# A decoder layer on one core: delays of the norm chains, an overlap of two of them, and the place of a weight cast

## The chip, the core and the metric

The kernel runs on one core of a Trainium2 chip. A core has five engines, each with its own instruction stream: TensorE (PE: matrix products, with weight loads shown apart as PEld), VectorE (DVE), ScalarE (ACT), GpSimd (POOL) and SyncE (SP), whose stream here mostly issues DMA transfers. An engine runs its stream in order and waits on semaphores for the others. The metric is the device time of one execution in microseconds; smaller is better.

## What is computed

One inference step of one decoder layer, for a prompt of 1024 tokens and a sample group of 8 x 8 = 64 tokens that share the weights; together 1088 columns of 1024 values. All data is float32.

```python
def rmsnorm(x, g):
    y = x32 * lax.rsqrt(jnp.mean(x32 * x32, axis=-1, keepdims=True) + NORM_EPS)
    return (y * g.astype(jnp.float32)).astype(x.dtype)
def swiglu(x, w_gu, w_down):
    gate, up = jnp.split(x @ w_gu, 2, axis=-1)
    return (jax.nn.silu(gate) * up) @ w_down
def macaron_half(x, g_pre, w_gu, w_down, g_post):
    return x + 0.5 * rmsnorm(swiglu(rmsnorm(x, g_pre), w_gu, w_down), g_post)
...
hp = macaron_half(hp, ffn1_...)                       # FFN 1, width 2752
fq, fk, fv, lf, gq, gk, gv, gg, la = project(rmsnorm(hp, mix_norm_pre[l]), w_in[l], ...)
fo = fox_prompt(fq, fk, fv, lf)                       # forgetting attention, 8 heads x 64
go, s_p = gla_prompt(gq, gk, gv, la)                  # gated linear attention, 4 heads
hp = hp + rmsnorm(merge(fo, go, gg, gla_norm[l], w_out[l]), mix_norm_post[l])
hp = macaron_half(hp, ffn2_...)                       # FFN 2
```

The sample group goes through the same layer, with a paged cache of keys and values for its attention. Outputs are both groups' results and the new keys, values, gates and states.

## The kernel before

Activations lie transposed: 128 features to a partition block, eight blocks `k` (`KB`), tokens along the free axis. Tokens are cut into the chunks `CH` (0-256, 256-512, 512-768, 768-1088). Weights come through a `Feed`: a DMA brings a raw tile `wr`; ScalarE casts it to a high part `wh`, VectorE subtracts to get a low part `wl` (line 202 for both), and a product is three matmuls, `wh` by the activations' high part (`ua`, `ub`, `hh`), `wh` by the low part (`hl` and the like) and `wl` by the high part (line 219). `Feed.pump(ahead)` casts ahead of need; `ahead` is by default `NW` = 3 tiles, counted from the last one given free, and raw loads run ahead of the casts by `NRAWW` = 2.

The stages on TensorE in order, by the span's time: FFN 1 in two halves of the columns (to about 770 us); the combined projection of the first 512 columns, with units of 128 outputs each (770 to 935); the same for the other columns with attention interleaved (to 1126, the rest to 1219); the product with `w_out`, which runs among the last units; FFN 2 of the first half, with the sample group's paged attention beside it; and FFN 2 of the second half, from about 1890 to the end, in a form with seven products instead of eight for each pair of blocks (`job_seven`, the "sevens").

The order is set when the program is built. The main line is a list of jobs. Beside it run generators, the side chains: each `yield d` asks to be taken up again `d` microseconds later on a planner's clock, which counts the matmuls emitted (`tick`). One list, `quick`, is stepped whenever due; of the other, `side`, only the first entry is stepped, so the chains in it follow one another. What is emitted at a step takes its place in the engines' order close to where the main line then stands.

A norm chain (`norm`) is such a generator: squares on ScalarE, their sum `ss` on VectorE and GpSimd (line 318), a product with ones that gives a column of sums `ncol` (line 333), the power -1/2 on GpSimd, a diagonal `dg` on VectorE (line 375), a product with ones that spreads it over all rows, `nrows` (line 382), and then eight multiplications, each with its residual (lines 422 and 423) or its split into high and low parts (lines 445 to 448). A chain with `post` and `pre` does both norms one after the other. `DROWS` = 2 is the delay between diagonal and `nrows`, `DREDUCE` = 6 the one ahead of the second `ncol`. The chain behind FFN 1 has the key "p"; the chain `w0` between the `w_out` product and FFN 2 has the key "f2", and `first` of FFN 2 waits for it chunk by chunk (`need`).

A projection unit's result leaves its PSUM bank by `proj_evac`. For the value heads of both attentions ("V units") ScalarE copies it to a staging tile `st` (line 932; a ring of five), the chain yields, then TensorE turns it by transposes (line 937), and copies and DMAs follow (lines 944 and 955).

In the sevens the eighth step of a pair (`third`) adds the product to `sg` (line 696), which empties a PSUM bank, and for the last block of a group the operations silu, product, `hh` and `hl` follow (lines 705 to 709). The down products come next; VectorE adds their banks to `y` (line 629).

Of the kernel before, what the change touches and what calls it, by code (L numbers as in the profile page):

```python
# [33 lines left out]
NW = 3  # L34
# [4 lines left out]
STEP = 2.0  # L39
DREDUCE = 6.0  # L40
DROWS = 2.0
COL = 0.42e-3


# [125 lines left out]
class Step:  # L170
    def __init__(self, ctx, tc, A, O):
        self.ctx, self.tc, self.nc, self.A, self.O = ctx, tc, tc.nc, A, O
        nc = self.nc
        self.const = ctx.enter_context(tc.tile_pool(name="const", bufs=1))
        self.dram = ctx.enter_context(tc.tile_pool(name="dram", bufs=1, space=DRAM))
        self.n = 0
        self.side, self.quick, self.bg, self.pend = [], [], [], []
        self.ncw, self.ssb, self.xb = NCW, 3, 2
        self.ready = set()
        self.kept, self.later = False, []  # L180
        self.last, self.pin = {}, True
        self.calm, self.haste = False, 0.0
        self.held = False
        self.rate = self.due = self.now = 0.0
        self.banks = dict(col=("col", 1), col2=("col", 1), rows=("rows", 1))
        cp = self.const
        self.ident = cp.tile([P, P], F32, name="ident")
        make_identity(nc, self.ident)
        self.ones = cp.tile([P, P], F32, name="ones")
        nc.vector.memset(self.ones, 1.0)  # L190
        self.mhalf = cp.tile([P, 4], F32, name="mhalf")
        nc.vector.memset(self.mhalf, -0.5)
        self.gain = cp.tile([P, 6, KB], F32, name="gain")
# [193 lines left out]
        while key not in self.ready:  # L387
            self.step_side(True)

    def norm(self, y, y0, c0, n, pool, post=None, pre=None, v=None, key=None):  # L390

        nc = self.nc
        rows = lambda k: y[:, k, c0 - y0:c0 - y0 + n]
        if v is None:
            sums = []
            for k in range(KB):
                self.square(rows(k), k, n, pool, sums)
            v = [self.rms(sums, n, pool, "col2")]
        if post:
            gi, res, out = post  # L400
            xs = []

            def fetch():
                k = 2 * len(xs)
                if k < KB:
                    xs.append(pool.tile([P, 2, self.ncw], F32, name=self.uid("x"), tag="x", bufs=self.xb))
                    nc.sync.dma_start(xs[-1][:, :, :n], res[:, k:k + 2, c0:c0 + n])
            for _ in range(self.xb):
                fetch()
        while not v:  # L410
            yield
        yield self.haste / 3 or 2.0
        dg = self.rms_diag(v[0], pool)
        yield self.haste / 3 or DROWS
        if post:
            rb = self.rms_rows(dg, n)
            self.held = self.haste > 0
            sums = []
            for k in range(KB):
                if k and k % 2 == 0:  # L420
                    yield
                nc.vector.scalar_tensor_tensor(out=rows(k), in0=rows(k), scalar=self.gain[:, gi, k:k + 1], in1=rb[:, :n], op0=ALU.mult, op1=ALU.mult)
                (nc.gpsimd if k % 2 else nc.vector).tensor_tensor(out=rows(k), in0=rows(k), in1=xs[k // 2][:, k % 2, :n], op=ALU.add)
                if k % 2:
                    fetch()
                if k % 4 == 3:
                    s = slice(k - 3, k + 1)
                    nc.sync.dma_start(out[:, s, c0:c0 + n], y[:, s, c0 - y0:c0 - y0 + n])
                if pre is not None:
                    self.square(rows(k), k, n, pool, sums)  # L430
            if pre is None:
                self.ready.add((key, c0))
                return
            yield DREDUCE
            v = self.rms(sums, n, pool, "col2")
            yield 1.0
            dg = self.rms_diag(v, pool)
            yield DROWS
        rb = self.rms_rows(dg, n)
        xh, xl, o = self.at(c0)  # L440
        for k in range(KB):
            if k and k % 2 == 0:
                yield
            yk = rows(k)
            nc.vector.scalar_tensor_tensor(out=yk, in0=yk, scalar=self.gain[:, pre, k:k + 1], in1=rb[:, :n], op0=ALU.mult, op1=ALU.mult)
            uh, ul = xh[:, k, o:o + n], xl[:, k, o:o + n]
            nc.scalar.copy(uh, yk)
            (nc.gpsimd if k % 2 else nc.vector).tensor_tensor(out=ul, in0=yk, in1=uh.bitcast(F32), op=ALU.subtract)
        self.ready.add((key, c0))
# [73 lines left out]
    def ffn(self, w_gu, w_dn, f):  # L523
# [168 lines left out]
        def job_seven(g, hb, i, z, w):  # L692

            n = f.n // 2
            a, b = slice(0, n), slice(n, 2 * n)
            add = lambda out, x, y: self.keep(nc.vector.tensor_tensor(out=out, in0=x, in1=y, op=ALU.add))  # L696
            if i == 0:
                if hb == g[0]:
                    make(g)
                sg(hb)  # L700
                z.up = f.H.tile([P, 2 * n], F32, name=self.uid("up"), tag="up", bufs=1)
                z.turn, self.kept = 0, True
                z.q, z.u, z.v = f.temps
            t, up = sgs[hb], z.up
            silu = lambda c: self.keep(nc.scalar.activation(out=t[:, c], in_=t[:, c], func=AF.Silu))
            mul = lambda c: self.keep(nc.vector.tensor_tensor(out=t[:, c], in0=t[:, c], in1=up[:, c], op=ALU.mult))
            hh, hl = hid[hb]
            high = lambda c: self.keep(nc.scalar.copy(hh[:, c], t[:, c]))
            low = lambda c: self.keep(nc.vector.tensor_tensor(out=hl[:, c], in0=t[:, c], in1=hh[:, c].bitcast(F32), op=ALU.subtract))  # L709
            whole, last = slice(0, 2 * n), hb == g[-1]  # L710
            self.calm = not last and i >= 2
            if i == 0:
                seven(z, w, 0, "b11", lambda ps: self.keep(nc.scalar.copy(z.q, ps)))
                seven(z, w, 1, "t2", lambda ps: add(z.u, z.q, ps))
            elif i == 1:
                seven(z, w, 1, "t3", lambda ps: add(z.v, z.u, ps))

                def both(ps):
                    add(z.u, z.u, ps)
                    add(up[:, b], z.v, ps)  # L720
                seven(z, w, 0, "t1", both)
            elif i == 2:
                def first(ps):
                    add(t[:, a], z.q, ps)
                    if last:
                        silu(a)
                seven(z, w, 0, "b21", first)

                def second(ps):
                    add(up[:, a], z.v, ps)  # L730
                    if last:
                        for fn in (mul, high, low):
                            fn(a)
                seven(z, w, 1, "t4", second)
            else:
                def third(ps):
                    add(t[:, b], z.u, ps)
                    if last:
                        for fn in (silu, mul, high, low):
                            fn(b)  # L740
                    else:
                        self.later += [lambda fn=fn: fn(whole) for fn in (silu, mul, high, low)]
                seven(z, w, 0, "b22", third)
            self.flush()
# [51 lines left out]
        for g, chunks, kind in f.plan:  # L796
# [8 lines left out]
            elif kind == "last":  # L805
                up4 = [gu(2 * hb - 1 + i) for hb in g for i in range(2)]
                dn = [[w_dn[d2][:, 2 * P * g[0]:2 * P * (g[-1] + 1)] for d2 in d] for d in ((0, 1), (2, 3))]
                reqs = up4[:3] + [(r, f.place(i)) for i, r in enumerate([up4[3]] + dn)]
# [26 lines left out]
    def work(self, jobs):  # L835
        self.feed = Feed(self, [r if isinstance(r, (tuple, Sums)) else (r, None) for rs, *_ in jobs for r in rs])
        for reqs, fn, early in jobs:
            ws = [self.feed.get() for _ in reqs]
            self.feed.pump()
            fn(*ws)  # L840
            self.feed.free(len(reqs) - early)
        self.flush()


# [25 lines left out]
class StepA(Step):  # L870
# [35 lines left out]
    def proj_evac(self, u, c0, n, pt):  # L906
# [8 lines left out]
        elif u < U_GATE:  # L915
            i = u - U_FQ if u < U_FK else u - U_FK
# [13 lines left out]
        elif U_FV <= u < U_GG or u >= U_GV:  # L930
            s = st(F32)
            nc.scalar.copy(s[:, :n], pt)
            yield 3.0
            tp = self.mm(512)
            bl = blocks(c0, n)
            for j, (o, w) in enumerate(bl):
# [4 lines left out]
            if u >= U_GV:  # L941
                i = u - U_GV
# [8 lines left out]
            else:  # L951
                i = u - U_FV
# [8 lines left out]
        else:  # L961
            i, dst, sc = (u - U_GQ, self.gqs, 0.125) if u < U_GK else (u - U_GK, self.gks, 1.0)
# [358 lines left out]
class StepB(StepA):  # L1321
# [432 lines left out]
    def whole(self):  # L1754
# [19 lines left out]
        y0 = F.tile([P, KB, HALF], F32, name="y0")  # L1774
# [164 lines left out]

        jobs += j2[:UNITS0] + [([], start3, 0)] + j2[UNITS0:]  # L1940
        j3 = self.proj_jobs(ORDER1, lambda j: CH[2:], hook3)
        w0 = Part(y0=0, after=lambda c0, n, v: self.norm(p3.y, 0, c0, n, w0.N, (3, self.h1, self.h2), 4, v, "f2"))
        p4 = Part()

        def mid3():
# [122 lines left out]
f='float32'  # L2068
# [37 lines left out]
```

## Time and profile before

| | us |
|---|---|
| median of 3 runs (lowest to highest) | 2300.27 (2299.33 to 2301.25) |
| profiled execution | 2296.98 |
| its span | 2295.2 |
| TensorE busy | 2233.1 (97%) |
| VectorE busy | 1523.3 (66%) |
| ScalarE busy | 1017.9 (44%) |
| GpSimd busy | 685.6 (30%) |

The mean granted clock of TensorE was 0.994 of full speed. Times in the views are counted from the span's start. A row of the timeline gives start, duration, engine, line, operation, output and inputs, the count where several are put together, and in brackets the idle time ahead with the instruction that ended it. Line numbers in the rows are those of the kernel before.

### The profile page before, as it was taken

What the parts mean: (1) busy time and instruction counts of PE and PEld (TensorE: products, weight loads), DVE (VectorE), ACT (ScalarE), POOL (GpSimd) and SP (SyncE); (2) the same over time, 40 slices, a digit from 0 to 9 for tenths busy, and PEclk for the clock granted to TensorE, in tenths of its full rate; (3) what the DMA queues carried; (4) which work ended last, traced back from release to release, by engine and by line L of the source; (5) the groups of instructions that cost most, each with busy time, mean ns of one, the idle gap of its engine ahead of it and who ended that gap; (6) DMA issues with size and microseconds to landing.
All of it is one profiled execution on the core that took longest, in us unless ns stands there. A gap on an engine that the chain in (4) does not pass through costs nothing.

```text
span 2295.2 us, 40073 instructions
## 1 busy us (share of the span) xinstructions
PE 2233.1 (97%) x15004; PEld 1984.3 (86%) x15004; DVE 1523.3 (66%) x2670; ACT 1017.9 (44%) x1748; POOL 685.6 (30%) x639
## 2 busy tenths in 40 slices
PE   7999999999999999999999999999999999999999
PEld 6998898999999877889897667777777989999998
DVE  7677787877778774576345333348774688778766
ACT  5443444533344565655344312236555545334432
POOL 3333332432223231011323444731110134334413
PEclk9999999999999999999999999999999999999999
DMA  6233333322334566563556899875545554234324
GB/s 212 87 97 93 105 102 120 102 79 92 93 111 138 184 226 192 174 191 122 187 154 211 293 328 307 294 211 147 149 137 152 183 178 127 93 96 134 106 79 138
DMA packets 199427, 357.22 MB, mean 156 GB/s; under 512 B 27265, under 2 KB 102594, under 8 KB 198850
## 3 DMA queue, kind: packets, MB, share of 16 engines
q1 hardware_dynamic: 187570, 316.38, 44.0%
q0 software_dynamic: 11664, 38.28, 4.9%
q8 instruction: 119, 1.95, 0.3%
q14 instruction: 74, 0.61, 0.1%
HBM read 308.93 MB, written 45.65 MB: 154 GB/s over the span
## 4 chain that ended last, share of the span: by engine, by line
PE 72%; DVE 12%; issue 6%; ACT 4%; DMA 4%; POOL 2%; SPq 1%; DVEq 0%; POOLq 0%; ACTq 0%
PE mm L219 45%; PE mm L681 14%; DVE wl L202 4%; PE mx L681 2%; PE po L1428 1%; ACT wh L202 1%; PE sp L1169 1%; PE po L1207 1%; PE tp L1412 1%; PE pa L1561 1%; PE s L1394 1%; DVE qd L1520 1%; DVE hl L709 1%; PE s L1395 1%; DVE fm L1399 0%
## 5 line engine op out<-in xcount | busy, mean ns | idle before, releaser
L219 PE MATMUL mm<-ua,wh 128*128 128x512 f32 (+1 forms) x1488 | 459.6, 392 | 3.2 <-ACT ua L202 1.8
L202 DVE TENSOR_TENSOR wl<-wr,wh 128x1024 fp32r<-128x1024 f32 (+1 forms) x249 | 290.6, 1167 | 174.3 <-ACT wh L202 172.1
L202 ACT CAST wh<-wr 128x1024 fp32r<-128x1024 f32 (+1 forms) x249 | 245.6, 986 | 312.8 <-PE mm L219 228.7
L219 PE MATMUL mm<-ub,wh 128*128 128x320 f32 (+2 forms) x1600 | 332.2, 302 | 0.0
L219 PE MATMUL mm<-hl,wh 128*128 128x256 f32 (+2 forms) x1006 | 331.0, 331 | 0.1
L219 PE MATMUL mm<-hh,wh 128*128 128x256 f32 (+2 forms) x958 | 320.8, 337 | 7.9 <-DVE sg L696 4.6
L219 PEld LDWEIGHTS mm<-ua,wh 128*128 128x128 f32 x1488 | 269.6, 193 | 64.6 <-issue 16.3
L219 PE MATMUL mm<-hh,wl 128*128 128x256 f32 (+2 forms) x958 | 316.6, 331 | 2.2 <-DVE wl L202 2.2
L219 PE MATMUL mm<-ua,wl 128*128 128x512 f32 (+1 forms) x736 | 281.2, 383 | 0.4 <-DVE wl L202 0.4
L219 PEld LDWEIGHTS mm<-ub,wh 128*128 128x128 f32 (+1 forms) x1600 | 255.3, 189 | 6.2 <-issue 4.4
L681 PE MATMUL mm<-ub,wh 128*128 128x288 f32 (+1 forms) x1328 | 258.3, 290 | 0.0
L219 PE MATMUL mm<-ub,wl 128*128 128x320 f32 (+1 forms) x784 | 232.0, 296 | 0.0
L629 DVE TENSOR_TENSOR y<-y,mm 128x256 f32<-128x256 f32 (+2 forms) x275 | 137.1, 525 | 119.7 <-PE mm L219 118.8
L681 PEld LDWEIGHTS mm<-ub,wh 128*128 128x128 f32 x1328 | 210.9, 189 | 0.0
L219 PEld LDWEIGHTS mm<-hh,wh 128*128 128x128 f32 x958 | 180.8, 189 | 30.0 <-DVE sg L696 5.9
L219 PEld LDWEIGHTS mm<-hl,wh 128*128 128x128 f32 x1006 | 189.8, 189 | 15.2 <-issue 1.1
L219 PEld LDWEIGHTS mm<-hh,wl 128*128 128x128 f32 x958 | 181.0, 189 | 19.4 <-DVE wl L202 3.7
L681 PE MATMUL mm<-ub,wl 128*128 128x288 f32 (+1 forms) x664 | 192.8, 290 | 0.0
L681 PE MATMUL mm<-ua,wh 128*128 128x288 f32 (+1 forms) x912 | 177.6, 290 | 0.0
L219 PEld LDWEIGHTS mm<-ua,wl 128*128 128x128 f32 x736 | 141.4, 193 | 28.8 <-issue 2.7
L1088 POOL DMA_INDIRECT pr<-in_cv,rows x128 | 129.7, 1013 | 106.9 <-PE sp L1169 32.0
L219 PEld LDWEIGHTS mm<-ub,wl 128*128 128x128 f32 x784 | 148.0, 189 | 0.2 <-issue 0.2
(324 smaller groups left out, 4229.5 us busy)
## 6 DMA issues: line engine op xcount, KB each, us to landing
wr<-in_wgu SPq DMA_DIRECT2D x72, 512.0 KB
wr<-in_wd SPq DMA_DIRECT2D x68, 512.0 KB
pr<-in_ck SPq DMA_DIRECT2D x112, 256.0 KB
wz<-in_wgu SPq DMA_DIRECT2D x100, 256.0 KB
wr<-in_win SPq DMA_DIRECT2D x50, 512.0 KB
wx<-in_wgu SPq DMA_DIRECT2D x50, 256.0 KB
wr<-in_wout SPq DMA_DIRECT2D x24, 512.0 KB
wr<-in_wd SPq DMA_DIRECT2D x40, 256.0 KB
```

What stands on the lines that cost most here:

```text
L202: for ins in (self.nc.scalar.copy(hi, src), self.nc.vector.tensor_tensor(out=lo, in0=src, in1=hi.bitcast(F32), op=ALU.subtract)):
L219: ins = self.nc.tensor.matmul(*a, **kw)
L629: self.note(nc.vector.tensor_tensor(out=yk, in0=yk, in1=pds[d2, c0, e], op=ALU.add))
L681: nc.tensor.matmul(ps, a, x, start=(k == 0 and j == 0), stop=(k == KB // 2 - 1 and j == len(ops) - 1))
L709: low = lambda c: self.keep(nc.vector.tensor_tensor(out=hl[:, c], in0=t[:, c], in1=hh[:, c].bitcast(F32), op=ALU.subtract))
L1088: nc.gpsimd.indirect_dma_start(out=raw[:, i], out_offset=None, in_=A["ck" if kind == "K" else "cv"].rearrange("g p n -> (g p) n"), in_offs ...
L1169: nc.tensor.matmul(sp[32 * a:32 * a + 32, 256 * hf:256 * hf + 256], qz[p % 2][:, a, s, :], raw[:, :, a * P:(a + 1) * P], start=False, stop ...
L1207: nc.tensor.matmul(po[r], pT[:, t, r], raw[:, :, a * P:(a + 1) * P], start=(t == 0), stop=False)
L1394: nc.tensor.matmul(sp[:, o:o + m], qa[:, qs], ka[:, o:o + m], start=True, stop=False)
L1395: nc.tensor.matmul(sp[:, o:o + m], qb[:, qs], kb[:, o:o + m], start=False, stop=not end)
L1412: nc.tensor.transpose(tp[:, k * P:(k + 1) * P], p[:, (k0 + k) * P:(k0 + k + 1) * P], self.ident)
L1428: nc.tensor.matmul(out, v[:, k, r], pT[:, k, s], start=(k == 0 or (k == 1 and not one)), stop=(k == last or (k == last - 1 and not one)))
```

## The change

Four things change. A norm chain with key "p" waits `DPROJ` = 4 planner microseconds between diagonal and `nrows`, both times, in place of 2. V units wait 5 in place of 3 between copy and transposes. The chain `w0` gets `over`: after the first norm's results are out, it moves the next chain that waits in `side` over to `quick`, so that the second chunk's chain is stepped beside the rest of the first. And at the last block of a group's step 2 (`second`), in the half with `f.end`, `pump` and `free` look ahead `NW - 1` = 2 tiles only, so that one cast pair is emitted a job later.

```diff
+DPROJ = 4.0
...
+        self.near = None
...
-    def norm(self, y, y0, c0, n, pool, post=None, pre=None, v=None, key=None):
+    def norm(self, y, y0, c0, n, pool, post=None, pre=None, v=None, key=None, over=False):
...
-        yield self.haste / 3 or DROWS
+        rest = DPROJ if key == "p" else DROWS
+        yield self.haste / 3 or rest
...
+            if over and len(self.side) > 1:
+                self.quick.append(self.side.pop(0))
             yield DREDUCE
...
-            yield DROWS
+            yield rest
...
             self.calm = not last and i >= 2
+            self.near = NW - 1 if f.end and last and i == 2 else None
...
-            self.feed.pump()
+            self.feed.pump(self.near)
             fn(*ws)
-            self.feed.free(len(reqs) - early)
+            self.feed.free(len(reqs) - early, self.near)
...
             nc.scalar.copy(s[:, :n], pt)
-            yield 3.0
+            yield 5.0
...
-        w0 = Part(y0=0, after=lambda c0, n, v: self.norm(p3.y, 0, c0, n, w0.N, (3, self.h1, self.h2), 4, v, "f2"))
+        w0 = Part(y0=0, after=lambda c0, n, v: self.norm(p3.y, 0, c0, n, w0.N, (3, self.h1, self.h2), 4, v, "f2", True))
```

No instruction is added or taken away on any engine apart from the program's own bookkeeping; rows change their places. Three places follow. Line numbers of the changed kernel are up to six higher.

The first is VectorE in the second group of the last FFN half, from the last block's first adds to the first down tile's banks (`wl` is a weight tile's low part, `y` the FFN's output). Before:

```order
L709 TENSOR_TENSOR hl_20985<-sg_21386,hh_20984 128x288
L202 TENSOR_TENSOR wl_21494<-wr_21422,wh_21493 128x1024
L696 TENSOR_TENSOR sg_21386<-y_9261,mm_21508 128x288
L706 TENSOR_TENSOR sg_21386<-sg_21386,up_21387 128x288
L709 TENSOR_TENSOR hl_20985<-sg_21386,hh_20984 128x288
L202 TENSOR_TENSOR wl_21527<-wr_21459,wh_21526 128x1024
L629 TENSOR_TENSOR y_19338<-y_19338,mm_21530 128x256
```

After:

```order
L714 TENSOR_TENSOR hl_20985<-sg_21386,hh_20984 128x288
L701 TENSOR_TENSOR sg_21386<-y_9261,mm_21493 128x288
L711 TENSOR_TENSOR sg_21386<-sg_21386,up_21387 128x288
L714 TENSOR_TENSOR hl_20985<-sg_21386,hh_20984 128x288
L204 TENSOR_TENSOR wl_21512<-wr_21422,wh_21511 128x1024
L204 TENSOR_TENSOR wl_21516<-wr_21459,wh_21515 128x1024
L634 TENSOR_TENSOR y_19338<-y_19338,mm_21530 128x256
```

The first of the two casts moved from between the two columns' operations to behind both, and the two casts now stand next to each other ahead of the `y` add.

The second is TensorE where the projection ends (`ub` operands) and FFN 2 begins (`mm_13430`, `ua` operands), with the second chunk's `ncol` and `nrows`. Before:

```order
L219 MATMUL mm_13329<-ub_104,wl_13193 128x320
L333 MATMUL ncol_2158_13380<-ones,ss_13242 128x2 x2
L219 MATMUL mm_13430<-ua_99,wh_13284 128x256
L219 MATMUL mm_13430<-ua_100,wh_13284 128x256
...
L382 MATMUL nrows_13388<-dg_13386,ones 128x128 x2
L219 MATMUL mm_13430<-ua_99,wl_13285 128x256
```

After:

```order
L221 MATMUL mm_13207<-ub_104,wl_13037 128x320
L335 MATMUL ncol_2140_13239<-ones,ss_13003 128x2 x2
L221 MATMUL mm_13207<-ub_104,wh_13036 128x320
...
L384 MATMUL nrows_13293<-dg_13265,ones 128x128 x2
L221 MATMUL mm_13285<-ub_104,wh_13166 128x320
...
L221 MATMUL mm_13430<-ua_99,wh_13329 128x256
```

Before, `ncol` stood directly ahead of the FFN's first matmul and `nrows` eight matmuls inside it. Now `ncol` stands 99 gemm matmuls ahead of that first matmul and `nrows` 69, and 30 lie between the two.

The third is ScalarE in the first projection, where the last chunk's norm (squares, lines 314 and 316) meets the first V unit's copy (`st`, lines 932 and 938). Before:

```order
L314 ACTIVATE sq_8899<-y_113 128x320
L314 ACTIVATE sq_8907<-y_113 128x320
L920 ACTIVATE st_8920<-mm_8843 128x512
L926 COPY st_8926<-mm_8843 128x512
L314 ACTIVATE sq_8955<-y_113 128x320
L314 ACTIVATE sq_8960<-y_113 128x320
L202 CAST wh_9029<-wr_8914 128x1024
L314 ACTIVATE sq_8977<-y_113 128x320
L314 ACTIVATE sq_8984<-y_113 128x320
L932 COPY st_8997<-mm_8916 128x512
L955 COPY st_9017<-mm_9011 128x512
```

After:

```order
L926 ACTIVATE st_8893<-mm_8831 128x512
L204 CAST wh_8952<-wr_8829 128x1024
L932 COPY st_8899<-mm_8831 128x512
L316 ACTIVATE ss_8941<-y_113 128x320
L316 ACTIVATE ss_8935<-y_113 128x320
L938 COPY st_8962<-mm_8889 128x512
L204 CAST wh_9017<-wr_8887 128x1024
L316 ACTIVATE sq_8966<-y_113 128x320
L316 ACTIVATE sq_8974<-y_113 128x320
```

The V unit's copy stood behind all eight squares of the chunk and stands now behind the first two. On TensorE the chain's `nrows` moved 27 matmuls of 512 columns later there, and the V unit's four transposes 9 of them later; the next chain's `nrows` (the second norm of the same chunk) comes 38 matmuls later.

## The prediction

> **What bounds the kernel now.** I read the page first, then TensorE's waits in total, then the timelines around the largest of them. The page's head, busy times and granted clock:
>
> ```profile
> span 2295.2 us, 40073 instructions
> PE 2233.1 (97%) x15004; PEld 1984.3 (86%) x15004; DVE 1523.3 (66%) x2670; ACT 1017.9 (44%) x1748; POOL 685.6 (30%) x639
> PEclk9999999999999999999999999999999999999999
> ```
>
> TensorE is busy for 2233.1 of 2295.2 us. The kernel is bound by it nearly everywhere, and no rearrangement that leaves the matmuls as they are can win more than the 62.1 us of idle time plus what short half-clock stretches cost. So the question is which of its waits the change touches. The view of TensorE's waits (microseconds in total, how often, longest one):
>
> ```profile
> PE nrows L382 <- DVE dg L375: 5.8, 4, 2.4
> PE mm L219 <- DVE sg L696: 4.6, 4, 1.8
> PE ncol L333 <- DVE ss L318: 4.6, 4, 1.9
> PE mm L937 <- ACT st L932: 2.6, 1, 2.6
> PE mm L219 <- DVE y L629: 1.3, 2, 1.1
> PE s L1394 <- DMA ka<-ks: 1.2, 1, 1.2
> ```
>
> These are small lists: four times a norm's `nrows` product waited for VectorE's diagonal, four times a norm's `ncol` for its sum, four times a down product for VectorE to empty a bank (`sg` L696), once a transpose for ScalarE's copy. The change works on just these. A result counts as no change within 0.2%, which is 4.6 us and about what a measurement of this kernel can tell.
>
> **The change part by part.**
>
> *Cast of the second down tile (`near`).* It acts on the five groups of the last FFN half (the only one with `f.end`). TensorE's rows at the four groups that wait, and in the second one what VectorE and ScalarE do around it:
>
> ```profile
> 1964.30 0.41 PE L219 MATMUL mm<-hh,wh 128*128 128x320 f32 x1 [1.13 <-DVE sg L696]
> 2036.52 0.41 PE L219 MATMUL mm<-hh,wh 128*128 128x320 f32 x1 [0.63 <-DVE sg L696]
> 2110.09 0.41 PE L219 MATMUL mm<-hh,wh 128*128 128x320 f32 x1 [1.76 <-DVE sg L696]
> 2181.93 0.41 PE L219 MATMUL mm<-hh,wh 128*128 128x320 f32 x1 [1.13 <-DVE sg L696]
> ...
> 2033.91 0.46 DVE L709 TENSOR_TENSOR hl<-sg,hh 128x288 fp32r<-128x288 f32 x1 [0.50 <-ACT hh L708]
> 2034.87 1.23 DVE L202 TENSOR_TENSOR wl<-wr,wh 128x1024 fp32r<-128x1024 f32 x1 [0.50 <-ACT wh L202]
> 2036.02 0.44 DVE L696 TENSOR_TENSOR sg<-y,mm 128x288 f32<-128x288 f32 x1
> 2038.88 1.23 DVE L202 TENSOR_TENSOR wl<-wr,wh 128x1024 fp32r<-128x1024 f32 x1 [0.49 <-ACT wh L202]
> 2040.02 1.14 DVE L629 TENSOR_TENSOR y<-y,mm 128x256 f32<-128x256 f32 x3
> ...
> 2033.79 1.05 ACT L202 CAST wh<-wr 128x1024 fp32r<-128x1024 f32 x1
> ...
> 2040.49 0.39 PE L219 MATMUL mm<-hh,wh 128*128 128x256 f32 x1
> ```
>
> The bank that TensorE needs is emptied by the add at 2036.02. That add stands on VectorE behind the cast of 1.23 us, and the cast waited 0.50 for ScalarE's half of it. The four waits add up to 1.13 + 0.63 + 1.76 + 1.13 = 4.65 us. With the cast gone from there, the add can follow the operation of 2033.91 directly. The cast's row and the add's overlap by 2034.87 + 1.23 - 2036.02 = 0.08; with the same overlap the add would start at 2033.91 + 0.46 - 0.08 = 2034.29, which is 1.73 earlier, and the wait goes.
>
> What is late next: both casts now stand in a row behind the block's last operation, ahead of the `y` add that empties the banks of the first down tile. The cast at 2038.88 would start 1.73 earlier, at 2037.15; two of them, at the 1.14 from start to start that the rows of 2038.88 and 2040.02 show, put the `y` add at 2037.15 + 2 x 1.14 = 2039.43, only 0.59 earlier than now. TensorE's next down tile starts at 2040.49, on the heels of that add. So a group gains some 0.59 and not its whole wait; 4 x 0.59 = 2.4 us. The ends are 4.65 (the bank freed at 2040.02 turns out not to be needed at once) and 0 (ScalarE's two casts come later than I assume). I take 2.4, since the rows of 2040.02 and 2040.49 stand so close. The fifth group has no such wait and costs nothing.
>
> *Two norm chains overlap (`over`, ahead of the second FFN).* TensorE, then VectorE, then two stretches with the granted clock (the third number from the end):
>
> ```profile
> 1219.72 0.61 PE L333 MATMUL ncol<-ones,ss 128*128 128x2 f32 x4 [1.30 <-DVE ss L318]
> 1221.92 1.04 PE L382 MATMUL nrows<-dg,ones 128*128 128x128 f32 x4 [0.54 <-DVE dg L375]
> ...
> 1219.24 0.43 DVE L318 TENSOR_TENSOR ss<-ss,sq 128x256 f32<-128x256 f32 x1
> 1221.35 0.43 DVE L375 TENSOR_TENSOR dg<-ident,nv 128x256 f32<-128x256 f32 x1 [0.82 <-POOL nv L364]
> ...
> 1222.10:1225.60 3.50, 3.50 (x18) 3.50 (x18) 3.10 (x7) 0.41 (x1) 0.00 (x0) 0.51 0.41 109
> 1225.60:1229.00 3.40, 3.40 (x31) 3.40 (x31) 1.26 (x4) 2.79 (x8) 1.65 (x3) 1.00 0.39 95
> ```
>
> The second chunk's chain now ends directly ahead of the FFN's first product, with nothing left for TensorE to do meanwhile: 1.30 + 0.54 = 1.84 us of idle time, and behind it 3.5 us at a clock of 0.51, in which 18 matmuls ran where the next 3.4 us hold 31. Those 18 would have taken 18 x 3.4 / 31 = 2.0, so the half clock cost about 1.5. Afterwards the chain's `ncol` has 99 gemm matmuls behind it before the FFN starts, and 30 of them stand between it and its `nrows`; at 3.4 / 31 = 0.11 us each `ncol` comes some 11 us ahead of the FFN, and the 30 between the two last 3.3 us, more than the 1221.92 - 1219.72 = 2.2 that the chain took from the one to the other. Cover: the rest of the projection. I count the whole, 1.84 + 1.5 = 3.3 us; the ends are 3.3 and 0 (a chain that waits as long in its new place).
>
> [...]
>
> *Rows and turning with more delay in the first projection (`DPROJ`, and 5 for 3 in `proj_evac`).* TensorE, VectorE and ScalarE:
>
> ```profile
> 822.88 0.91 PE L382 MATMUL nrows<-dg,ones 128*128 128x128 f32 x6 [2.04 <-DVE dg L375]
> 838.01 0.66 PE L937 MATMUL mm<-ident,st 128*128 128x128 f32 x4 [2.62 <-ACT st L932]
> 838.96 0.40 PE L219 MATMUL mm<-ua,wl 128*128 128x512 f32 x1
> 839.66 0.39 PE L219 MATMUL mm<-ua,wl 128*128 128x512 f32 x1
> ...
> 821.65 1.08 DVE L375 TENSOR_TENSOR dg<-ident,nv 128x384 f32<-128x384 f32 x1
> ...
> 836.65 0.83 ACT L314 ACTIVATE sq<-y 128x320 f32<-128x320 f32 x2 [1.32 <-DVE st L1014]
> 837.39 0.57 ACT L932 COPY st<-mm 128x512 f32<-128x512 f32 x1
> ```
>
> Three matmuls of 512 columns take 839.66 - 838.96 = 0.70, 0.233 each. The order puts `nrows` 27 of them later (12 of the unit it stood in and 15 of the next), 6.3 us; the diagonal was ready 2.04 too late, so some 4 us of slack remain. The first transposes move 9 matmuls later, 2.1 us, and their copy (837.39, which stood behind eight squares of the norm that themselves waited for VectorE) now has only the first two squares ahead of it. Both waits should go: 2.04 + 2.62 = 4.66 us. The ends are 4.7 and 0 (ScalarE's copy late again). I take 4.7: each cover is twice the wait or better.
>
> What is queued behind: the last norm chain's `nrows` comes 38 matmuls later in the order, 38 x 0.233 = 8.9 us, less the 4.7 won, so about 4.2 later in time. It holds a buffer pool that the attention's tiles take over. GpSimd's clearing, the queue's first load behind it and the next wait:
>
> ```profile
> 860.96 2.17 POOL L1356 CAST kb<-zero 64x512 fp32r<-64x512 f32 x2
> ...
> 868.85 0.42 SPq L1327 DMA_DIRECT2D gnorm<-in_gnorm  x1
> 874.13 0.59 SPq L1375 DMA_DIRECT2D kb<-ks  x1
> ...
> 876.28 0.47 PE L1394 MATMUL s<-ka,qa 128*128 128x128 f32 x2 [1.17 <-DMA ka<-ks]
> ```
>
> Clearing would end at 863.13 + 4.2 = 867.3; SP's load of `kb` would be due at 874.13 - 4.7 = 869.4. SP's order up to there is set by the weight tiles and is nearly the old one, so it moves with TensorE. Hidden by 2.1 us, which is thin.
>
> *The same delay in the two chains of FFN 1's tail.* The rows it moves past:
>
> ```profile
> 728.58 0.42 PE L219 MATMUL mm<-hh,wh 128*128 128x320 f32 x1 [1.08 <-DVE y L629]
> 740.71 0.58 PE L333 MATMUL ncol<-ones,ss 128*128 128x2 f32 x4 [0.68 <-DVE ss L318]
> ```
>
> These may vanish (+1.76). But the chains' eight multiplications and splits now fall on other down products, whose banks VectorE empties; a wait of the kind at 728.58 can come back once per chain, 2 x 1.08 = 2.2. Between +1.8 and -2.2 I take 0.
>
> *The other V units* (the delay holds for all) change TensorE's order by a few rows without a wait that I can see to go: 0, bounded by the slower rival below. DMA counts, matmul counts and queues' loads are the same; SP's rows move by a few places.
>
> **Sum.** 2.4 + 3.3 + 4.7 + 0 = 10.4 us. The profiled execution took 2296.98 us (span 2295.2 and 1.8 around it), 3.3 below the median of 2300.27; 2296.98 - 10.4 = 2286.6 there, and 2300.27 - 10.4 = 2289.9 for the median.
>
> **The rivals.** *What the projection wins is given back at the next load.* If the last chain slips by the 2.1 us more that the clearing has in hand, the loads behind it on SP hold TensorE at the row now at 876.28, whose wait grows from 1.17 by up to 4.7. For it: that wait exists already. Against it: SP's rows are paced by weight tiles. Gain 5.7, time 2294.6.
>
> *The half clock stays, or returns elsewhere.* The wait goes but a stretch of 0.51 is met at some other place: 1.5 less, 2291.4; twice, 2292.9. For it: the stretches follow short gaps, and other gaps stay.
>
> *The waits only move.* The chains wait just as long in new places, and the casts alone count: 2297.9, no change. For it: VectorE is 66% busy and a chain's length is its own. Against it: the counted matmuls above.
>
> *Slower: the staging ring.* A V unit holds one of the five `st` buffers from its copy to its transposes, now for 2 us more of planned time. If that makes a later unit's copy late, TensorE waits for the bank:
>
> ```profile
> L932 ACT COPY st<-mm x24: 367/428/588, 837.4 to 1192.0; 128x512 f32<-128x512 f32 x8, 128x256 f32<-128x256 f32 x8, 128x320 f32<-128x320 f32 x8
> ```
>
> 24 copies at up to 0.588 us: one such wait each is 24 x 0.59 = 14.2, against a gain of 10.4, that is +3.8: 2304.1. From 0.63 us a unit on, the kernel is slower by over 0.2%. Against it: only the first of the 24 had a wait for ScalarE of over 2 us, and the others fall where TensorE waits little.
>
> **How the numbers follow.** Forecast 0.50; loads give it back 0.18; half clock 0.10; waits only move 0.14; ring 0.08. The forecast and the half clock are faster; the loads' case at 2294.6 lies 1.1 inside the limit of 2295.7, so I count 0.10 of its 0.18 as faster and 0.08 as no change; the ring is slower. Faster 0.70, same 0.22, slower 0.08. The best case is 4.65 + 3.3 + 4.7 + 1.8 = 14.5, or 2285.8; I start the range at 2285.5. Upward it takes in the loads' case and waits that only move, 2297.9 with 1 us of room: 2299. Outside stay the ring and a little of each other case. The forecast's own range, with the small parts at their ends, is 2286 to 2293.
>
> **What would show it.** Right: no wait for `sg` in the four groups, and the `y` add about 0.6 us earlier behind its group's first down product; no `ncol` or `nrows` wait between 1210 and 1220, and a clock of 1.00 there; no wait at the last chunk's `nrows` and the first V transposes. Wrong: a wait for `y` of a microsecond in the four groups, a wait for `ka` or `kb` of over 3 us, a row with `st` behind many transposes, or new waits for `y` in FFN 1's tail.

## The result, and the profile after

The changed kernel's median is 2292.41 us (2291.40 to 2294.12, 7 runs) against 2300.27 (2295.55 to 2301.25, 7 runs): 0.9976 of the time before, interval 0.9967 to 0.9986. That is 7.9 us between the medians; by the ratio, which is not formed from these two medians, it is 5.5 us, and 3.2 to 7.6 by the interval. The interval's lower end lies inside the 4.6 us that the prediction counts as no change. The forecast was 2289.9. The profiled execution's span is 2290.5 us, 4.7 less than before. The page's head:

```profile
span 2290.5 us, 40083 instructions
PE 2231.0 (97%) x15004; PEld 1983.1 (87%) x15004; DVE 1532.2 (67%) x2670; ACT 1016.9 (44%) x1748; POOL 690.1 (30%) x639
```

TensorE runs the same 15004 matmuls and is still the bound. What changed is its list of waits (us, times, longest):

```profile
PE mm L221 <- DVE y L634: 6.4, 11, 1.3
PE nrows L384 <- DVE dg L377: 3.9, 2, 2.4
PE ncol L335 <- DVE ss L320: 3.2, 2, 2.5
PE mm L221 <- ACT wh L204: 1.6, 2, 1.3
PE s L1400 <- DMA ka<-ks: 1.2, 1, 1.2
PE mm L221 <- ACT st L955: 1.0, 1, 1.0
PE mm L943 <- ACT st L938: 0.9, 1, 0.9
PE mm L221 <- DVE sg L701: 0.5, 1, 0.5
```

Of the four `sg` waits one of 0.5 is left (4.6 before), `nrows` fell from 5.8 to 3.9, `ncol` from 4.6 to 3.2, the V copy from 2.6 to 0.9. But `y` L634 grew from 1.3 to 6.4, 3.7 of it in the last FFN half, and waits of 1.3 for a weight cast and 1.0 for `st` L955 are new. The wait for `ka` stayed at 1.2, so the first rival did not come.

To see where time went, I cut every trace at the starts of six matmuls that each program has: the first product of the sevens (line 681) in FFN 1's second half, the first 512-column `mm<-ua,wh` of the projection, the first `s<-ka,qa`, the last 512-column `mm<-ua,wh` ahead of FFN 2, the first product of the paged attention (`sp<-pr,qz`), and the last half-tile product of FFN 2's second half (`mm<-hh,wt`). A stage is the difference of two starts, in us; the last one ends at the start of the last matmul:

| kernel | FFN 1's tail, to the projection | first projection, to `s<-ka,qa` | around the overlap, to the paged attention | FFN 2's last stretch, to the end |
|---|---|---|---|---|
| before | 363.07 | 105.40 | 78.75 | 375.68 |
| changed | 364.32 | 101.84 | 75.77 | 375.79 |
| cast only (`e1_near`) | 363.02 | 105.28 | 78.69 | 375.88 |
| cast between add and product (`e2_near_mid`) | 362.88 | 105.96 | 77.14 | 372.50 |
| rows' delay only (`e3_dproj`) | 364.40 | 103.41 | 77.17 | 376.20 |
| V units' delay only (`e4_vdelay`) | 362.98 | 105.40 | 79.12 | 375.12 |
| overlap only (`e5_over`) | 362.81 | 105.67 | 74.80 | 375.95 |
| changed, again (`e6_after_again`) | 364.34 | 101.90 | 75.39 | 375.99 |
| changed, rows' delay from column 512 on (`e7_no_tail_delay`) | 363.04 | 101.61 | 75.88 | 375.89 |
| best (`e8_best`) | 363.05 | 101.21 | 75.95 | 372.20 |
| changed, V units' delay 3 (`e9_after_v3`) | 364.34 | 103.71 | 74.99 | 376.25 |
| best, V units' delay 5 in the first projection only (`e10_best_v_first`) | 363.02 | 101.43 | 74.89 | 371.79 |
| best, again (`e11_best_again`) | 363.13 | 102.16 | 75.58 | 371.98 |

So in the changed kernel the first projection won 3.6 us, the stretch around the overlap 3.0, the last half nothing, and FFN 1's tail lost 1.3. That is 5.2 won in these stages; outside them 0.4 went in this pair of traces: 0.5 ahead of the tail, 1.8 between the paged attention and the last stretch and 0.4 behind the last matmul were lost, and 2.3 won between `s<-ka,qa` and the overlap. Stretches at half clock did not fall alike in the two traces: the granted clock was 0.66 from 1125 to 1130 us in the one before, and 1.00 from 1126 to 1130 in the changed kernel's.

### The profile page after: what moved, and what is told of

Its sections match the earlier page's. It is cut to its first block, busy times and chain, and to the rows that moved or that the text cites. A ratio compares the mean times of both kernels' runs of the same rounds, so it can differ in the third digit from the quotient of the medians.

```text
span 2290.5 us, 40083 instructions
## 1 busy us (share of the span) xinstructions
PE 2231.0 (97%) x15004; PEld 1983.1 (87%) x15004; DVE 1532.2 (67%) x2670; ACT 1016.9 (44%) x1748; POOL 690.1 (30%) x639
## 4 chain that ended last, share of the span: by engine, by line
PE 45%; DVE 8%; issue 5%; DMA 4%; ACT 3%; POOL 1%; SPq 0%; ACTq 0%; DVEq 0%; POOLq 0%
PE mm L221 29%; PE mm L686 3%; DVE wl L204 3%; PE mx L686 2%; PE po L1434 1%; DMA wr<-in_wd 1%; PE sp L1175 1%; PE tp L1418 1%; PE po L1213 1%; PE pa L1567 1%; ACT wh L204 1%; PE s L1400 1%; DMA wr<-in_wout 1%; DMA pr<-in_cv,rows 1%; PE s L1401 1%
## 5 line engine op out<-in xcount | busy, mean ns | idle before, releaser
L634 DVE TENSOR_TENSOR y<-y,mm 128x256 f32<-128x256 f32 (+2 forms) x275 | 137.3, 525 | 114.2 <-PE mm L221 113.3
```

The source lines that it names most:

```text
L634: self.note(nc.vector.tensor_tensor(out=yk, in0=yk, in1=pds[d2, c0, e], op=ALU.add))
```

## The experiments

The kernels of one group ran on one chip. The first four met a chip on which the paged attention alone, from its first to its last product, took 311 to 316 us where it takes 268 to 273 on the others. The kernel before was slow there too, by its times (median 2337.86 us). The ratios of this group are wide, so I read its stages, none of which holds the paged attention.

### Each part alone

The cast only, with the overlap off and both delays as before (against the changed kernel, as in every cut of code below):

```diff
-        rest = DPROJ if key == "p" else DROWS
+        rest = DROWS
...
-            yield 5.0
+            yield 3.0
...
-        w0 = Part(..., 4, v, "f2", True))
+        w0 = Part(..., 4, v, "f2"))
```

> Only the move of the cast in the last FFN half; delays and the overlap are as before. Theory: the waits for sg L696 (4.6 us, 4) go, but the moved cast lets its raw weight tile go later, so the next raw tile lands later and its cast stands ahead of the y adds of the second down tile; TensorE then waits for y twice in a group (about 0.7 and 0.35 us). Over the four groups nothing is won, within 0.6 us, and the time stays within 0.1% of before. Rival (the prediction's sum): the y adds come 0.59 us earlier and that is kept, 2.4 us less in all.

Measured: 1.0007 of the time before (0.9990 to 1.0023); the last stretch 375.88 against 375.68. Nothing is won, as the theory said. The second group in the changed kernel shows why: VectorE, ScalarE, SyncE's loads, then TensorE.

```profile
2028.80 0.46 DVE L714 TENSOR_TENSOR hl<-sg,hh 128x288 fp32r<-128x288 f32 x1 [0.50 <-ACT hh L713]
2029.17 0.45 DVE L701 TENSOR_TENSOR sg<-y,mm 128x288 f32<-128x288 f32 x1
2032.04 2.36 DVE L204 TENSOR_TENSOR wl<-wr,wh 128x1024 fp32r<-128x1024 f32 x2 [0.49 <-ACT wh L204]
2034.31 1.15 DVE L634 TENSOR_TENSOR y<-y,mm 128x256 f32<-128x256 f32 x3
2038.04 1.23 DVE L204 TENSOR_TENSOR wl<-wr,wh 128x1024 fp32r<-128x1024 f32 x1 [2.19 <-ACT wh L204]
2039.18 0.75 DVE L634 TENSOR_TENSOR y<-y,mm 128x256 f32<-128x256 f32 x2
...
2036.96 1.05 ACT L204 CAST wh<-wr 128x1024 fp32r<-128x1024 f32 x1 [4.00 <-DMA wr<-in_wd]
...
2033.29 1.46 SPq L121 DMA_DIRECT2D wr<-in_wd  x2
...
2034.88 0.36 PE L221 MATMUL mm<-hh,wh 128*128 128x256 f32 x1 [0.30 <-DVE y L634]
2039.65 0.41 PE L221 MATMUL mm<-hh,wh 128*128 128x320 f32 x1 [0.36 <-DVE y L634]
```

The add that empties the bank follows directly (2029.17), and the first `y` add starts 5.51 after the `hl` of 2028.80; before it was 2040.02 - 2033.91 = 6.11. So the 0.60 that the prediction worked out did come. It is then given back. There are two raw buffers, and a load into one is issued when VectorE's half of its cast is done: the one of 2033.29 right behind the first of the two subtractions of 2032.04 (2032.04 + 1.23 = 2033.27). Both subtractions stand late now, so the third tile's cast waits 4.00 us for that load and starts at 2036.96. Its second half stands on VectorE at 2038.04, ahead of the second down tile's `y` adds, and TensorE waits a second time in the group. In the last half the views of ScalarE's and TensorE's waits of the changed kernel have

```profile
ACT wh L204 <- DMA wr<-in_wd: 19.1, 5, 4.0
PE mm L221 <- DVE y L634: 3.7, 8, 0.7
```

The kernel before has no such wait of `wh` there: a late load in each of the five groups. On TensorE the eight waits for `y` (0.70 and 0.36, 0.30 and 0.36, 0.70 and 0.33, 0.70 and 0.26 in the four groups) and one of 0.49 for `sg` in the third, 4.2 in all, stand in place of the 4.65. The waits ahead of the first down tile shrank by 1.8, and the second ones, which are new, take 1.3 of that back.

To tell this from a bound in VectorE's work itself, the next kernel lets the first raw tile go earlier. It puts the cast between the last block's second add and its product:

```diff
                     add(t[:, b], z.u, ps)
                     if last:
+                        if f.end:
+                            self.feed.pump()
                         for fn in (silu, mul, high, low):
```

> Only a cast's place in the last FFN half: it is put between the last block's second add to sg and the product that follows it, so the bank is emptied early and the raw tile is let go about when it was before. Theory of the late raw tile: the sg waits go (4.6 us), the y adds of the first down tile come 0.6 to 0.95 us earlier, and no second wait for y follows; 2.4 to 3.8 us less than before. Rival (the down products are bound by VectorE's work in that stretch whatever the order): the waits only change their names, less than 1 us gained.

Measured: 0.9988 of the time before (0.9973 to 1.0004, on that chip); the last stretch 372.50, 3.2 less than before, inside what the theory said. VectorE in the same group:

```profile
2077.91 0.45 DVE L701 TENSOR_TENSOR sg<-y,mm 128x288 f32<-128x288 f32 x1
2078.49 1.23 DVE L204 TENSOR_TENSOR wl<-wr,wh 128x1024 fp32r<-128x1024 f32 x1
2079.63 0.45 DVE L711 TENSOR_TENSOR sg<-sg,up 128x288 f32<-128x288 f32 x1
2081.53 1.22 DVE L204 TENSOR_TENSOR wl<-wr,wh 128x1024 fp32r<-128x1024 f32 x1 [0.49 <-ACT wh L204]
2082.68 1.14 DVE L634 TENSOR_TENSOR y<-y,mm 128x256 f32<-128x256 f32 x3
2084.41 1.23 DVE L204 TENSOR_TENSOR wl<-wr,wh 128x1024 fp32r<-128x1024 f32 x1 [0.20 <-ACT wh L204]
2085.96 0.78 DVE L634 TENSOR_TENSOR y<-y,mm 128x256 f32<-128x256 f32 x2 [0.32 <-PE mm L221]
```

The cast fills the time in which VectorE waits for ScalarE's silu. The add is early, the casts do not stand next to each other, the third cast starts 1.73 after the `y` adds (3.73 in the changed kernel), and the `y` adds of 2085.96 wait for TensorE and not the other way. The raw tile goes earlier too: the load that follows the subtraction of 2078.49 is issued at 2079.74, 3.6 ahead of its cast, which waits for TensorE and not for it. In the last half ScalarE still waits for loads, 7.7 us in four waits against 19.6 with the cast moved alone, but TensorE's waits for `y` are down to 0.7. So the late load is seen in the rows, but this kernel changes VectorE's order as well as the load, and its 3.2 us cannot be shared out between the two. A third raw buffer, which would change the load alone, was not run.

The rows' delay only:

> Only the longer delay ahead of the spread products of the chains behind FFN 1. Theory: in FFN 1's tail 1.4 us are lost (new waits for y L634 of about 1.0 and 1.3 us and one for a weight cast of 1.3 us), and in the projection both large waits go (2.0 for nrows and 2.6 for the V unit's copy), since with this delay alone the copy stands behind two squares only; in all 2.5 to 3.5 us less. Rival (the V units' own delay removes their wait): only the 2.0 of nrows goes, the wait of 2.6 for the copy stays, and the time is 0.6 us less than before.

Measured: 0.9995 (0.9979 to 1.0011); tail 364.40, 1.3 lost; first projection 103.41, 2.0 won, so 0.7 in all. The `nrows` wait is gone. The V unit's copy moved up ahead of six squares, but TensorE still waits for it, less and twice:

```profile
836.99 0.66 PE L943 MATMUL mm<-ident,st 128*128 128x128 f32 x4 [1.52 <-ACT st L938]
843.71 0.66 PE L943 MATMUL mm<-ident,st 128*128 128x128 f32 x4 [0.61 <-ACT st L938]
```

These 1.52 + 0.61 = 2.13 stand against 2.62, so neither theory was right: the order of ScalarE is this delay's doing, but it saves only 0.5, since the first squares wait for the norm's later rows (4.75 us, for `y` of L426).

The V units' delay only:

> Only the longer delay between a V unit's copy and its transposes. Theory: the order of ScalarE is unchanged, the first copy stays behind eight squares, but the transposes come later in TensorE's order by two planner microseconds, so the wait of 2.62 us for the copy shrinks by some 2; the other V units gain or lose under 0.5 us; in all 1.5 to 2.5 us less. Rival: the transposes' delay pushes results into the staging ring and TensorE waits at later units, no gain or a loss of over 1 us.

Measured: 1.0011 (0.9994 to 1.0027); the first projection 105.40, as before. TensorE's waits, and the granted clock (third from the end) right behind the first of them:

```profile
822.77 1.11 PE L384 MATMUL nrows<-dg,ones 128*128 128x128 f32 x6 [2.05 <-DVE dg L377]
841.77 0.83 PE L335 MATMUL ncol<-ones,ss 128*128 128x2 f32 x6 [1.01 <-DVE ss L320]
...
824.00:828.00 4.00, 4.00 (x13) 3.11 (x13) 4.00 (x9) 0.51 (x2) 1.15 (x2) 0.66 0.99 268
```

The copy's wait of 2.62 went, one of 1.01 for the chain's sum came in its place, and a stretch of reduced clock stands here (0.66 over these 4 us) that the kernel before does not have. The three other kernels with the old order in this place have the stretch too; with the cast only:

```profile
823.30:826.70 3.40, 3.40 (x12) 2.92 (x12) 3.40 (x6) 1.24 (x2) 0.00 (x0) 0.50 0.98 238
838.30 0.66 PE L943 MATMUL mm<-ident,st 128*128 128x128 f32 x4 [1.05 <-ACT st L938]
```

Their waits for the copy are 1.05, 1.30 and 1.23 in place of 2.62: the copy is late by ScalarE's own order, and TensorE's matmuls, slower at the clock of 0.50, fill a part of the wait. Their stages, 105.28, 105.96 and 105.67, are those to compare with. So alone this delay is worth -0.1 to 0.6 us in the first projection; what it is worth alone at full clock, no run shows.

The overlap only:

> Only the overlap of the two norm chains ahead of FFN 2. Theory: the wait for ncol (1.30 us), the one for nrows (0.54) and the half clock behind them (1.5) go, 3.3 us between the start of the w_out product and the FFN; and since the V units are as before, the wait of 1.0 us that TensorE shows in the changed kernel at 1199.26 us for a V unit's copy (st L955) does not come. Rival: that wait comes with the overlap alone, because ScalarE then has both chains' squares and splits ahead of the copy; 2 us less in that stretch and not 3.3.

Measured: 0.9990 (0.9980 to 1.0000); the stretch 74.80, 4.0 less than before. Its chain's products run without a wait, and the wait for `st` is 0.28 at another copy, not 1.0 at L955:

```profile
1194.57 0.56 PE L221 MATMUL mm<-ub,wh 128*128 128x320 f32 x2 [0.28 <-ACT st L950]
1204.92 0.50 PE L335 MATMUL ncol<-ones,ss 128*128 128x2 f32 x4
1209.12 0.60 PE L384 MATMUL nrows<-dg,ones 128*128 128x128 f32 x4
```

How much of the 4.0 is the overlap's and how much the clock's, the kernel with the cast in the middle tells by chance. It has no overlap, and TensorE's waits there are those of before, but its clock is full:

```profile
1218.58 0.61 PE L335 MATMUL ncol<-ones,ss 128*128 128x2 f32 x4 [1.27 <-DVE ss L320]
1220.77 0.46 PE L384 MATMUL nrows<-dg,ones 128*128 128x128 f32 x2 [0.53 <-DVE dg L377]
...
1221.50:1225.00 3.50, 3.50 (x32) 3.50 (x30) 2.56 (x7) 1.93 (x6) 0.73 (x1) 1.00 0.45 128
```

Its stretch took 77.14, and that of the rows' delay alone, also at full clock, 77.17, against 78.69 to 79.12 in the other three without overlap. Each of those three has one half-clock stretch here (a mean clock of 0.94 from 1220 to 1250 us): 3.50 us at 0.51 lose 3.50 x 0.49 = 1.7 us, which is the difference. So the same waits are followed by a half-clock stretch in three executions of five, and in none of the eight with the overlap (74.80 to 75.95 us; in the changed kernel's trace the clock is 1.00 from 1200 to 1230). The overlap itself is worth 2.3 us (77.14 - 74.80), and 1.7 more in an execution in which such a stretch would have come.

### Parts undone, and a better kernel

The changed kernel once more, beside the next two:

> The changed kernel once more, as the measure for the two runs beside it. Theory and rival alike: 0.9965 to 0.9985 of the time before, and in the profile 1.4 us lost in FFN 1's tail, 3.7 us won in the first projection, nothing won in the last FFN half.

Measured: 2292.91 us, 0.9977 (0.9968 to 0.9986), with the stages of the first measurement (364.34, 101.90, 75.39, 375.99).

The rows' delay only from column 512 on, so that FFN 1's tail is as it was:

```diff
-        rest = DPROJ if key == "p" else DROWS
+        rest = DPROJ if key == "p" and c0 >= HALF else DROWS
```

> The changed kernel with the longer delay ahead of the rows only for the chunks from column 512 on, so that the chains in FFN 1's tail are as before. Theory: the 1.4 us lost there come back and the 3.7 us of the projection stay; 1.4 us less than the changed kernel. Rival: the projection's gain rests on the whole chain being later, so a part of it goes with the tail's delay.

Measured: tail 363.04, 1.3 won back, and the projection keeps its 101.61. The whole is 0.9973 (0.9961 to 0.9985), not told apart from the kernel beside it. What the tail had lost, in the changed kernel:

```profile
724.91 0.41 PE L221 MATMUL mm<-hh,wh 128*128 128x320 f32 x1 [0.98 <-DVE y L634]
729.61 0.42 PE L221 MATMUL mm<-hh,wh 128*128 128x320 f32 x1 [1.32 <-DVE y L634]
768.80 0.36 PE L221 MATMUL mm<-hh,wh 128*128 128x256 f32 x1 [1.29 <-ACT wh L204]
```

and with the delay undone there:

```profile
729.94 0.41 PE L221 MATMUL mm<-hh,wh 128*128 128x320 f32 x1 [1.08 <-DVE y L634]
742.05 0.58 PE L335 MATMUL ncol<-ones,ss 128*128 128x2 f32 x4 [0.66 <-DVE ss L320]
759.45 0.38 PE L221 MATMUL mm<-hh,wh 128*128 128x256 f32 x1 [0.29 <-ACT hh L204]
```

The later rows put the chain's multiplications ahead of the down tiles' `y` adds, and its squares ahead of a weight cast.

Both improvements together, with the overlap and the V units' delay:

> The overlap, both delays (the one ahead of the rows only from column 512 on), and the second down tile's cast between the last block's second add and its product. Theory: 1.4 us (tail) and 3.2 us (last FFN half) less than the changed kernel, about 0.995 of the time before. Rival: what is won ahead of the paged attention is lost at its gathers, and only the last half's 3.2 us show.

Measured: 2284.72 us, 0.9947 of the time before (0.9931 to 0.9963), against 0.9977 of the changed kernel on the same chip; the intervals do not meet. Tail 363.05 and last stretch 372.20: both gains are there in full.

Then the V units' delay undone in the changed kernel:

> The changed kernel with the V units' delay back at 3. Theory: in the first projection the wait for the first V unit's copy comes back in part (1.5 and 0.6 us, as with the rows' delay alone), 1.6 us more there; ahead of FFN 2 the wait of 0.5 to 1.0 us for the last V unit's small copy (st L955) goes; in all 0.5 to 1 us more than the changed kernel, 0.998 of the time before. Rival: the V units' delay does nothing beside the rows' delay, and the time is that of the changed kernel or less.

Measured: 0.9983 (0.9971 to 0.9994); first projection 103.71, 1.8 to 1.9 more than in the changed kernel, with the two waits of the rows' delay alone (1.46 and 0.61) and a longer one for `ka` (2.06). So this delay has its worth beside the other: 1.8 of the 3.6. It has its price too. Around the overlap this kernel took 74.99, against 75.77 and 75.39 with the delay: there TensorE's waits of 1.02 and 0.55 for `st` L955 are replaced by one of 0.45 for another copy.

Last, the delay of 5 in the first projection only:

```diff
-            yield 5.0
+            yield 5.0 if n == HALF else 3.0
```

> The best kernel so far with the V units' delay of 5 only in the first projection (512 columns wide) and 3 in the second. Theory: the wait for st L955 of some 1.0 us ahead of FFN 2 goes and the first projection keeps its gain; 1 us less than the kernel beside it, 0.9942 of the time before. Rival: with the overlap ScalarE is late there whatever the delay, and a wait of another V unit takes its place; no difference.

> The best kernel so far once more, as the measure for the run beside it: 0.993 to 0.9965 of the time before, with no wait for sg L701 in the four groups of the last half and none of 1.2 us for a weight cast in FFN 1's tail.

Measured: 0.9952 (0.9938 to 0.9965) with the delay in the first projection only, 0.9950 (0.9937 to 0.9964) for the best kernel beside it. The wait for `st` ahead of FFN 2 did go. In the best kernel's two executions it stands as

```profile
PE mm L221 <- ACT st L957: 1.1, 1, 1.1
PE mm L221 <- ACT st L957: 0.5, 1, 0.5
```

and with the delay in the first projection only, 0.14 for another copy is left. The stretch took 74.89 against 75.95 and 75.58, that is 0.7 to 1.1 less, as the theory had it, and the first projection kept its gain (101.43). The other executions with the overlap agree: 74.80 to 74.99 where it is 3 there, and 75.39 to 75.95 where it is 5. The time of the whole does not tell the two kernels apart.

## Why the prediction was right or wrong

The time, 2292.41, lies 2.5 above the forecast of 2289.9 and inside its range, and the sign was right. The places were right in two of three: the last FFN half gained nothing. No term came out above its size; the gain is 5.5 us by the ratio where 10.4 were forecast, and the range held it because it reached up to 2299, a gain of 1.3. The terms one by one:

- **The cast, 2.4 forecast, 0 measured** (375.68 to 375.79, and 375.88 alone). The step that failed is "a group gains some 0.59 and not its whole wait". The 0.60 was there at the first `y` add. I had not followed the raw buffer that the moved cast holds: the next load is late, its cast stands ahead of the next `y` adds, and TensorE waits a second time. The waits ahead of the first down tile shrank by 1.8, the second ones take 1.3 of it back, and the stage shows no gain. The lower end of 0 was in the range for another reason (ScalarE's casts), which is not what happened.
- **The overlap, 3.3 forecast, 3.0 measured in this pair of traces.** The waits went as worked out: `ncol` and `nrows` run without one. That is worth 2.3 with the old V delay, but 1.2 to 1.8 in the kernels with the new one (77.14 less 75.39 to 75.95): the wait for `st` L955 is a term that the prediction put at 0, under the other V units. The half clock, 1.5 forecast and 1.7 by the granted clock, was counted as certain. It came behind these waits in three executions of five, so as a mean it is about 1.0; the 3.0 rests on its having come in the trace of before, which is luck in part.
- **The first projection, 4.7 forecast, 3.6 measured.** `nrows` lost its whole wait of 2.04, as forecast. The first transposes wait no more, but the second ones now do, 0.87 us, and a first wait of 0.44 for `y` at the projection's start (772.62) is the tail's delay, since it is gone where that is undone:

```profile
843.81 0.66 PE L943 MATMUL mm<-ident,st 128*128 128x128 f32 x4 [0.87 <-ACT st L938]
```

  The step "each cover is twice the wait or better" looked at the first V unit only. The load of `ka` stayed hidden, as the 2.1 us in hand had it; its wait is 1.17 before and after.
- **FFN 1's tail, 0 forecast, 1.3 lost.** The loss is there in all four kernels with the delay in the tail and in none of the other nine. It lies between the bounds of +1.8 and -2.2; the cause named in the lower one, `y` adds behind the chain, is what the rows show, with a weight cast beside it.
- **The slower rival (the staging ring)** did not come. Its sign is there in small: with the delay, the wait for `st` L955 of 1.0 us ahead of FFN 2, against 0.28 with the overlap alone. The runs show that the delay brings it, and not whether a full ring is the reason.
- **The half clock as a rival** was right that such stretches are met at other places. From 1000 us on the trace before has five at a clock of 0.50, from 1126.5, 1222.1, 1549.8, 1618.1 and 1870.6, and the changed kernel's has five, from 1503.6, 1544.6, 1571.9, 1616.3 and 1865.4; those of 1503.6 and 1571.9 are new. Its reason, that they follow short gaps, is shown for most: eight of the ten start in a wait of TensorE of 0.54 to 2.96 us or within 1.7 us of its end. The stretch of 1616.3 has no wait in the 10 us ahead of it, and that of 1618.1 one of 0.69, 8.4 us ahead. Nor does a gap always bring one: waits of 1.27 + 0.53 us had no half clock behind them in one kernel, and 1.30 + 0.54 had 3.5 us of it in another. Ahead of FFN 2 it was there in none of the eight executions with the overlap.

The sum with measured terms is 0 + 3.6 - 1.3 and 1.2 to 1.8, that is 3.5 to 4.1 without a half-clock stretch that goes, and 5.2 to 5.8 with one. Both lie in the interval of 3.2 to 7.6.

## What to carry to other kernels

When a weight cast is moved later, follow its source buffer as well as its engines: with two raw tiles, the load two tiles on starts when this cast ends (issued at 2033.29 here, behind a subtraction that ended at 2033.27). A better place than behind everything is where the vector engine waits anyway, between two operations that pass through another engine; here that was worth 3.2 us where the later place was worth nothing. And a delay that helps in one stage should be set for that stage alone: the rows' delay lost 1.3 us in FFN 1's tail, and the V units' delay 0.4 to 1.1 us ahead of FFN 2.

## What was not expected of the hardware

With the same program order in that place and nearly the same waits (1.30 + 0.54 and 1.27 + 0.53 us), one execution had 3.5 us at a clock of 0.51 behind them and another had none (stretches of 78.75 and 77.14 us). A gain of 1 to 2 us that rests on one pair of traces can be this alone. A half-clock stretch need not cost its 1.7 us either: in the first projection the wait for ScalarE's copy behind it was the shorter (1.05 to 1.30 us in place of 2.62, and none with the V units' delay), and the stage was nearly as long as it was (105.40 without it, 105.28 to 105.96 with it). And one chip took 311 to 316 us for the paged attention that took 268 to 273 on the others, while the stretch from its last product to FFN 2's last stretch took 403 to 408 on all of them.
